# Matrix product with row normalisation: reordering VectorE's work around the start of the first two-block group

## The chip, the core and the metric

The kernel runs on one core of a Trainium2 chip. The metric is the device time of one execution in microseconds (us). A kernel's time is the median of its runs.

Engine names in the profile: PE is TensorE (matmuls), DVE is VectorE, ACT is ScalarE, POOL is GpSimd, and SPq is the queue on which SyncE issues DMAs.

## The reference

```python
def reference(a, b, gamma, eps):          # a, b: 2048 x 2048 fp32, gamma: 2048
    x = np.matmul(a, b)
    rms = np.sqrt(np.mean(x ** 2, axis=-1, keepdims=True) + eps)
    return (gamma * x / rms).astype(np.float32)
```

## The kernel before

The rows of `a` are 16 blocks of 128. A head computes blocks 0 to 3 while `b` arrives. From block 4 on the blocks go in groups of two (group 2 is blocks 4 and 5, and is called the first group, `G0`). Each half of a group's columns is computed with seven products in place of eight, in the manner of Strassen. A product is 8 matmuls of 128x512. Its left operand is either a quarter of the transposed block or a sum of two quarters (`s_1`, `s_2`, `s_5`, `s_6`, `s_7`, made on VectorE by `a_sums`). Blocks 2 and 3, called "the pair", already use the seven products for their right half. Their last additions are left over for the first group's time.

Each row block also needs a norm (`row_norm`, ScalarE), a factor from it (`row_factor`, VectorE), a scaling to fp16 (`row_apply`, ScalarE) and a transpose by DMA. Each engine works through its instructions in order. A hook is a place between two products where other work is put into the program. This is the end of the head:

```python
    p6 = new_bank()
    product(PAIR, 1, 6, p6)
    a_sums(G0, (5,))
    nc.vector.tensor_tensor(out=x22, in0=pair[1], in1=x22, op=ALU.subtract)
    for g in range(2):
        turn(HB + 1, g)                                     # TensorE transposes block 5
        take_transposed(HB + 1, g, turned[HB + 1, g], nc.vector.tensor_copy)
    square_half(0, 1)                                       # ScalarE
    square_half(1, 1)
    take_rms(0)                                             # VectorE sum (tot), ScalarE root (rms)
    a_sums(G0, (2, 1))

    def pair_sums():                                        # two additions of 128x512
        ...
    def pair_ends():                                        # two more; they empty p7 and p6
        ...
```

One half of a group, with the hooks:

```python
        product(g, j, *one)
        nc.scalar.copy(out=c, in_=one[1])                   # L591
        last_squares()
        at_hook(1)
        product(g, j, *two)
        nc.vector.tensor_tensor(out=t, in0=two[1], in1=c, op=ALU.add)      # L595
        at_hook(2)
        ...                                                 # product 1; L599
        product(g, j, 4, p2, start=False)                   # accumulates onto one/two's banks
        nc.scalar.copy(out=x21, in_=p2)                     # L602
        ...
        product(g, j, 3, p5, start=False)
        nc.scalar.copy(out=x12, in_=p5)                     # L607
        ...
```

The hooks of the first group that matter here (`nxt` is block 6). The second list belongs to its second half:

```python
            if g == G0:                                     # first half
                hook(0, finish, 0, (1,))                    # scale by gamma/rms, store
                hook(1, row_norm, nxt)
                hook(1, take_rms, 1)
                hook(2, row_factor, nxt)
                hook(2, finish, 0, (0,))
                hook(2, apply, nxt)                         # row_apply, then the transposing DMA
                hook(2, row_norm, nxt + 1)
                hook(2, a_sums, g, (7, 6))
                hook(2, finish, 1, (1, 0))
                hook(2, row_factor, nxt + 1)
                hook(2, pair_sums)
                hook(2, pair_ends)
                hook(4, apply, nxt + 1)
...
                hook(2, finish, r2, (1, 0))                 # second half: block 2's two stores
...
                hook(0, load_after, g, nxt + 2)             # load block 8, released by block 7's transpose
                if g == G0:
                    hook(2, wait_for, x_slot[HB + r2][:, 0:1])
                    hook(2, load_block, nxt + 3)            # load block 9
                    hook(5, row_norm, nxt + 2)              # norm of block 8, before the next group's L591
```

## Time and profile before

| | before |
|---|---|
| time, median of 3 runs (range) | 221.73 us (221.34 to 221.86) |
| span of the profiled run | 219.9 us |
| TensorE busy | 209.3 us (95%) |
| TensorE's one wait between 54 and 95 us | 0.5 us, for the sum `s_2` |

TensorE is the engine to watch. Once the first group runs, every product follows the last without a gap, and each takes 1.73 us (8 matmuls, 216 ns apart). A start that comes later than the previous start plus 1.73 us is therefore a wait. That is a stricter reading than the bracketed idle time, because a matmul's record lasts longer than its slot.

The prediction shows the lines around the one wait. First, ScalarE in order of time (start, length, engine, line, operation, tiles, and in brackets the idle time before it with what ended it):

```profile
91.24 1.06 ACT L219 ACTIVATE sq<-a 128x1024 bf16<-128x1024 f32 x1 [1.37 <-DMA a<-in_a_dram]
...
93.80 0.57 ACT L591 COPY x<-acc 128x512 f32<-128x512 f32 x1
```

L591 is the copy that the next group's fourth product needs. TensorE reaches that product here:

```profile
96.96 3.62 PE L285 MATMUL acc<-t_left,head_at 128*128 128x512 bf16 x16
```

### The profile page before, as it was taken

To read this page: it belongs to the slowest core of one execution; us is meant where nothing else is said; L and a number is where in the kernel's file an instruction comes from. 1 tells how busy PE (TensorE), PEld (TensorE's weight loads), DVE (VectorE), ACT (ScalarE), POOL (GpSimd) and SP (SyncE) were. 2 spreads that over 40 slices of the span, in tenths; PEclk is the share of its full clock that TensorE was granted. 3 is DMA by queue.
4 is the path that set the end of the run, shared out by engine and by line. 5 is a ranking of instruction groups with operands and counts; after the bars stand their busy time and mean duration, and the time that the engine had idled before them with its cause. 6 is when DMAs were issued, how large, how long until landed. Compare 5 with 4: busy or idle time off the path is not lost.

```text
span 219.9 us, 3044 instructions
## 1 busy us (share of the span) xinstructions
PE 209.3 (95%) x1032; PEld 97.4 (44%) x1032; DVE 165.9 (75%) x326; ACT 127.0 (58%) x263; POOL 36.3 (16%) x75
## 2 busy tenths in 40 slices
PE   7799999999999999999999999999999999999970
PEld 3344544444454444444444444444444444444440
DVE  1128799999889999979795639946695659787781
ACT  2110002920599898688745997289747996334471
POOL 7544443343020002100200002000200000000040
PEclk9999999999999999999999999999999999999996
DMA  7999999999929895948799049965699249145045
GB/s 157 164 203 206 199 206 208 212 206 228 409 76 362 291 293 118 358 176 230 213 300 405 3 93 265 351 247 95 156 294 405 42 100 364 73 174 210 1 171 212
DMA packets 36864, 46.60 MB, mean 212 GB/s; under 512 B 22256, under 2 KB 26352, under 8 KB 35568
## 3 DMA queue, kind: packets, MB, share of 16 engines
q0 software_dynamic: 10608, 23.86, 44.1%
q1 hardware_dynamic: 25824, 22.02, 33.5%
q10 hardware_dynamic: 416, 0.52, 0.7%
q8 instruction: 8, 0.13, 0.2%
q14 instruction: 8, 0.07, 0.1%
HBM read 34.60 MB, written 16.78 MB: 234 GB/s over the span
## 4 chain that ended last, share of the span: by engine, by line
PE 65%; DMA 23%; ACT 4%; POOL 2%; issue 1%; DVE 1%; ACTq 0%; POOLq 0%
PE acc L285 64%; DMA b<-in_b_dram 14%; DMA early<-in_a_dram 5%; DMA a<-in_a_dram 4%; ACT sq L219 2%; POOL b L102 1%; ACT at_even L192 1%; PE acc L790 1%; POOL early L106 1%; DVE s L260 1%; DVE at_even L192 0%; ACT x L729 0%; DVE x L551 0%; ACT norm L222 0%; ACT x L531 0%
## 5 line engine op out<-in xcount | busy, mean ns | idle before, releaser
L285 PE MATMUL acc<-b,s 128*128 128x512 bf16 x408 | 93.3, 379 | 0.5 <-DVE s L260 0.5
L285 PEld LDWEIGHTS <-s 128*128 128x128 f16 (+1 forms) x512 | 49.9, 98 | 60.4 <-DVE s L260 1.0
L388 PE MATMUL acc<-b,head_at 128*128 128x512 bf16 x176 | 43.2, 379 | 1.2 <-DMA b<-in_b_dram 1.2
L303 ACT ACTIVATE sq<-x 128x512 bf16<-128x512 f32 x53 | 33.4, 630 | 6.9 <-DVE x L722 3.0
L370 DVE SCALAR_TENSOR_TENSOR x<-x,r,gamma_sb 128x1024 f32<-128x1024 f32 x28 | 34.8, 1282 | 0.7
L219 ACT ACTIVATE sq<-a 128x1024 bf16<-128x1024 f32 x24 | 25.3, 1053 | 2.1 <-DMA a<-in_a_dram 1.5
L388 PEld LDWEIGHTS <-head_at 128*128 128x128 bf16 x176 | 16.9, 98 | 20.6 <-issue 1.6
L242 ACT ACTIVATE head_at<-a,s 128x2048 f16<-128x2048 f32 x10 | 20.0, 1998 | 3.3 <-DVE s L229 3.3
L102 POOL DMA_DIRECT2D b<-in_b_dram x32 | 17.2, 540 | 20.8 <-DMA b<-in_b_dram 15.0
L430 ACT COPY x<-acc 128x512 f32<-128x512 f32 x5 | 2.9, 582 | 24.7 <-PE acc L388 24.7
L285 PEld LDWEIGHTS <-head_at 128*128 128x128 f16 (+1 forms) x112 | 10.9, 98 | 13.2
L285 PE MATMUL acc<-early,head_at 128*128 128x512 bf16 x64 | 14.5, 379 | 0.0
L285 PEld LDWEIGHTS <-at_even 128*128 128x128 f16 x96 | 9.4, 98 | 11.3
L285 PE MATMUL acc<-early,s 128*128 128x512 bf16 x56 | 14.2, 379 | 0.0
L260 DVE TENSOR_TENSOR s<-head_at 128x1024 f16<-128x1024 f16 (+5 forms) x22 | 13.4, 635 | 0.1
L609 DVE TENSOR_TENSOR x<-x,x 128x512 f32<-128x512 f32 x9 | 6.2, 692 | 8.8 <-ACT x L607 8.3
L127 POOL COPY pace<-x 128x1 f32<-128x1 f32 x4 | 1.7, 413 | 66.7 <-DVE x L618 65.6
L591 ACT COPY x<-acc 128x512 f32<-128x512 f32 x9 | 5.2, 573 | 11.5 <-PE acc L285 11.5
L173 DVE COPY head_at<-tbank 128x1024 bf16<-128x1024 bf16 x7 | 4.8, 692 | 8.7 <-PE tbank L168 8.5
L285 PE MATMUL acc<-t_left,s 128*128 128x512 bf16 x48 | 11.3, 379 | 0.0
L774 POOL TENSOR_SCALAR x<-x,r 128x512 f32<-128x512 f32 x1 | 2.7, 2652 | 51.2 <-DVE r L346 51.2
L276 DVE TENSOR_TENSOR b<-b 128x1024 bf16<-128x1024 bf16 x16 | 10.8, 684 | 0.2
(113 smaller groups left out, 237.5 us busy)
## 6 DMA issues: line engine op xcount, KB each, us to landing
out_dram<-x SPq DMA_DIRECT2D x29, 512.0 KB, 3.8
a<-in_a_dram POOLq DMA_DIRECT2D x10, 1024.0 KB, 8.7
b<-in_b_dram POOLq DMA_DIRECT2D x32, 256.0 KB, 10.0
a<-in_a_dram POOLq DMA_DIRECT2D x4, 512.0 KB, 9.8
early<-in_a_dram POOLq DMA_DIRECT2D x7, 256.0 KB, 10.2
gamma_sb<-in_gamma_dram POOLq DMA_DIRECT2D x2, 512.0 KB, 8.3
out_dram<-x SPq DMA_DIRECT2D x3, 256.0 KB, 2.6
out_dram<-a SPq DMA_DIRECT2D x1, 512.0 KB, 3.3
```

Of the source, the lines that this page charges most:

```text
L102: nc.gpsimd.dma_start(out=raw[j][kp][:, t, :], in_=b[lo:lo + P, j * HALF:(j + 1) * HALF])
L173: nc.vector.tensor_copy(out=head_at[:, 2 * kp:2 * kp + 2, :, :], in_=view)
L219: nc.scalar.activation(out=junk, in_=a32[mb][:, h * HALF:(h + 1) * HALF], func=ACTF.Square, scale=2.0 ** -8, accum_out=n2[:, h:h + 1])
L242: nc.scalar.activation(out=a16[mb], in_=a32.pop(mb), func=ACTF.Copy, scale=factor.pop(mb))
L260: nc.vector.tensor_tensor(out=sum_of(g, s)[:, lo:hi, :], in0=x[:, lo:hi, :], in1=y[:, lo:hi, :], op=op)
L276: nc.vector.tensor_tensor(out=flat[:, 1:3, :], in0=flat[:, 1:3, :], in1=flat[:, 0::3, :], op=ALU.add)
L285: nc.tensor.matmul(bank, lhsT[:, kp, :], rhs, start=(start and kp == 0), stop=(kp == KP - 1), skip_group_check=not start)
L303: nc.scalar.activation(out=sq[:, 0:CH], in_=src, func=ACTF.Square, scale=inv_sqrt_n, accum_out=msq[mb][:, c:c + 1])
L370: nc.vector.scalar_tensor_tensor(out=x, in0=x, scalar=inverse_of[mb], in1=gamma_sb[:, h * HALF:(h + 1) * HALF], op0=ALU.mult, op1=ALU.mult)
L388: nc.tensor.matmul(bank, head_at[:, kt, r, :], head_rhs(c, kt), start=(kt == 0), stop=(kt == KT - 1))
L591: nc.scalar.copy(out=c, in_=one[1])
L609: nc.vector.tensor_tensor(out=t, in0=t, in1=x12, op=ALU.add)
```

## The change

The intent: let VectorE do the two sums that TensorE waits for before a subtraction that nobody waits for; use VectorE's wait for the next norm for the pair's sums; empty the pair's two banks sooner.

```diff
     a_sums(G0, (5,))
-    nc.vector.tensor_tensor(out=x22, in0=pair[1], in1=x22, op=ALU.subtract)
     for g in range(2):
         turn(HB + 1, g)
         take_transposed(HB + 1, g, turned[HB + 1, g], nc.vector.tensor_copy)
     square_half(0, 1)
     square_half(1, 1)
+    a_sums(G0, (2, 1))
+    nc.vector.tensor_tensor(out=x22, in0=pair[1], in1=x22, op=ALU.subtract)
     take_rms(0)
-    a_sums(G0, (2, 1))
...
                 hook(1, take_rms, 1)
+                hook(2, pair_sums)
                 hook(2, row_factor, nxt)
-                hook(2, finish, 0, (0,))
                 hook(2, apply, nxt)
                 hook(2, row_norm, nxt + 1)
                 hook(2, a_sums, g, (7, 6))
-                hook(2, finish, 1, (1, 0))
+                hook(2, pair_ends)
+                hook(2, finish, 0, (0,))
+                hook(2, finish, 1, (1,))
                 hook(2, row_factor, nxt + 1)
-                hook(2, pair_sums)
-                hook(2, pair_ends)
+                hook(2, finish, 1, (0,))
```

## The prediction

> **What bounds the kernel now.** I read the busy times first, then the chain that ended last, then TensorE's waits, and then the order of time around the one place where TensorE waits. The page's first part:
>
> ```profile
> PE 209.3 (95%) x1032; PEld 97.4 (44%) x1032; DVE 165.9 (75%) x326; ACT 127.0 (58%) x263; POOL 36.3 (16%) x75
> ```
>
> The last pieces of the chain before its long end (start, length, what; us):
>
> ```profile
> 68.54 0.06 DVE tot L335
> 68.60 0.67 DVE s L260
> 69.27 0.05 issue
> 69.32 141.76 PE acc L285 x656
> ```
>
> From 69.32 on, the chain is TensorE alone: 656 matmuls without one step to another engine. 141.76/656 is 216.1 ns each. The pace without waits can be read at the two products that start at 84.87 and end where the next starts at 88.32: 3.45 us for 16, or 215.6 ns. At that pace 656 would take 141.4 us, so at most 0.3 us of stall lies in all of that stretch. Whatever happens to VectorE and ScalarE after 69.32 is hidden as long as no matmul waits for it. TensorE's waits from 54 to 95 us have a single entry:
>
> ```profile
> PE acc L285 <- DVE s L260: 0.5, 1, 0.5
> ```
>
> In TensorE's order of time it is this (s_5's product of the first group, then s_2's, then s_1's, then two on the transposed block):
>
> ```profile
> 66.97 1.89 PE L285 MATMUL acc<-b,s 128*128 128x512 bf16 x8
> 69.32 1.90 PE L285 MATMUL acc<-b,s 128*128 128x512 bf16 x8 [0.46 <-DVE s L260]
> 71.06 1.89 PE L285 MATMUL acc<-t_left,s 128*128 128x512 bf16 x8
> 72.78 0.59 PE L285 MATMUL acc<-t_left,at_even 128*128 128x512 bf16 x2
> ```
>
> Eight matmuls from 66.97 at 0.2157 end their issue at 68.70; the next begins at 69.32. So the true loss is 0.62 us (the record shows 0.46 because a matmul's record outlasts its slot). That is the prize. VectorE there:
>
> ```profile
> 66.05 0.69 DVE L260 TENSOR_TENSOR s<-at_even 128x1024 f16<-128x1024 f16 x1 [0.21 <-ACT at_even L192]
> 66.66 0.68 DVE L551 TENSOR_TENSOR x<-acc,x 128x512 f32<-128x512 f32 x1
> 67.26 0.68 DVE L192 COPY at_even<-tbank 128x1024 f16<-128x1024 f16 x1
> 67.86 0.68 DVE L192 COPY at_even<-acc 128x1024 f16<-128x1024 f16 x1
> 68.46 0.14 DVE L335 TENSOR_REDUCE tot<-msq 128x1 f32<-128x5 f32 x1
> 68.57 1.29 DVE L260 TENSOR_TENSOR s<-at_even 128x1024 f16<-128x1024 f16 x2
> 69.78 0.16 DVE L346 RECIPROCAL r<-rms 128x1 f32<-128x1 f32 x1
> 69.97 1.28 DVE L370 SCALAR_TENSOR_TENSOR x<-x,r,gamma_sb 128x1024 f32<-128x1024 f32 x1
> 71.18 0.15 DVE L335 TENSOR_REDUCE tot<-msq 128x1 f32<-128x5 f32 x1
> 71.33 0.69 DVE L595 TENSOR_TENSOR t_first<-acc,head_at 128x512 f32<-128x512 f32 x1
> ```
>
> VectorE is never idle here, so anything put ahead of something else delays the latter by its step. Steps: 0.60 from one of these sums or copies to the next, 0.71 where it reads what its predecessor wrote (the two pair sums start at 78.46 and 79.17), 1.21 after a scaling of 128x1024.
>
> **What the Trainium skill says.** "TensorE: Matmul & The Clock Gate", section "Wait — 56ns, not 53.3ns?": 512-column matmuls start 215.7 ns apart when warm; the trace's 215.6 agrees, so TensorE has no slower pace to mend. "VectorE: DVE Perf Modes", section "The DRAIN you can't avoid": a semaphore between two instructions costs nothing extra. Here it differs: 0.71 against 0.60, and I use the trace. "Perfetto Trace Analysis", section "Matmuls": rotate groups through banks so that emptying one overlaps the next. The trace agrees that this works already: the pair's seventh product sits in its bank from 64 us until 79.78 (the first of the sums that end the pair) and TensorE never waits for it. Same page, section on DMA instructions of the Sync queue: the record covers the issue, not the data. Here the store issued at 71.29 has a record of 0.35 us and lands after 4.1.
>
> **The change, part by part.** No instruction is added or removed; 286 VectorE rows stand in both builds. TensorE's own order is the same. Three moves:
>
> (1) Head's end: s_2 and s_1 go ahead of the subtraction (L551) and of the row-0 sum of squares (tot).
> (2) Inside the group: the two pair sums go ahead of the next row factor, and the two pair ends ahead of three scalings.
> (3) On the Sync queue the transposing DMA of block 6 now comes before the store of row 0's left half, which came before it.
>
> (1) worked out. s_5 stays at 66.05. The first copy now waits for the transposes, whose records end at 66.68: 66.72. Second copy 67.32. s_2 reads it: +0.71, 68.03, done 68.71. The second product starts at about 68.78 instead of 69.32: gain 0.54, remaining wait 0.08. Then s_1 68.64, subtraction 69.25, tot 69.85 (before: 68.46). ScalarE takes row 0's root only after tot: 70.03 to 70.23 (before 68.64). So the reciprocal is at 70.27, the scaling 70.46, the second tot 71.67, and L595 runs 71.82 to 72.51 (before 71.33 to 72.02). L595 empties the bank onto which the fourth product accumulates. TensorE would be ready for that product at 68.78 + 2 x 1.73 = 72.24, but gets the bank at 72.57: a new wait of 0.33. Before it started at 72.78. The gain is now 0.21.
>
> (2) and ScalarE. ScalarE also loses 1.39 at that root, because its copy (L591), two squares and norm stand behind it in order. These are the lines that it then works through without a break:
>
> ```profile
> 72.64 2.00 ACT L242 ACTIVATE head_at<-a,s 128x2048 f16<-128x2048 f32 x1 [0.52 <-DVE s L229]
> 78.33 2.00 ACT L242 ACTIVATE head_at<-a,s 128x2048 f16<-128x2048 f32 x1
> 82.64 0.57 ACT L591 COPY x<-acc 128x512 f32<-128x512 f32 x1
> ```
>
> The pair sums (72.42, 73.13) fill VectorE until the norm, now at about 73.4; the factor's third step ends at 74.26, where it ended at 72.60. ScalarE's first L242 starts at 74.30 instead of 72.64, and all behind it shifts by 1.66. On VectorE s_7 and s_6 come at 74.43 and 75.03 (product 7 wants them at 76.03: fine), the pair ends at 75.64 and 76.24, scalings at 76.85 and 78.24, the second factor done 79.98: second L242 at 80.02 (+1.69). So L591, which copies the second half's first product, runs 84.33 to 84.90. That bank is wanted by the fourth product of the second half; before, TensorE started it at 84.87 with ScalarE done at 83.21. After, TensorE would be ready at 72.57 + 7 x 1.726 = 84.65 and starts at 84.95. So the 0.21 is gone again, and 0.08 more.
>
> (3) The store of row 0's left half is scaled at 76.85 to 78.13 and its SBUF half is written next by ScalarE's L607, which would come at 81.92. The Sync queue issues in order. Before, the block-6 transpose held it for 3.18 us (74.67 to 77.85, with a store in flight), elsewhere 1.9. It now starts at 76.33, so the store goes out between 78.3 and 79.6 and lands 2.9 to 3.5 us later, between 81.2 and 83. L607 is late by 0 to 1.1; I take 0.1 to 0.2, as fewer transfers are in flight at 76. That adds to the wait of L591.
>
> Sum: 0.62 removed; 0.08 + 0.33 + 0.30 + 0.15 = 0.86 new. Net +0.2 us: 221.73 + 0.2 = 221.9. After that the lag of 1.7 us drains where ScalarE waits anyway (the before trace shows it waiting 1.37 at 91.24, 2.10 at 110.97, 3.84 at 117.88), and TensorE's fourth product at 96.96 has its copy done at 94.37, 2.6 us ahead. The 7 us after the last matmul are untouched.
>
> **Rivals.** First, the intended one: the wait goes and nothing replaces it. Then 221.73 - 0.54 = 221.2. For it: the only recorded wait of TensorE vanishes. Against it: L595 had only 72.78 - 72.02 = 0.76 of slack, and loses 0.49 while TensorE comes 0.54 earlier. Second, the store is blocked by the transpose as long as before (3.18): L607 at 82.5, L591 at 84.9, TensorE at 85.55, 0.7 later than before: 222.4. If the block-7 transpose, now right behind the store of row 1, also lands late, the load behind it and row 8's norm delay the copy for the product at 96.96 by up to the 2.6 us slack: up to 0.5 more, 222.9. Third, earlier freed banks matter: speaks against it that no product waited for one of them; worth 0.
>
> **Range and chances.** The floor is 221.2 less a little run-to-run scatter (221.34 to 221.86 before); the blocked store gives the ceiling. Range 221.2 to 222.7. Two per cent is 4.4 us, seven times the whole wait at stake, so within 2% is nearly certain: 0.98, 0.01 on each side.
>
> **What would show it.** Right: no wait, or under 0.15, before s_2's product; a wait of about 0.3 before the fourth product with L595 as releaser; ScalarE's first L242 near 74.3; a wait for ScalarE's L591 near 84.9. Wrong: TensorE with no wait after 68.8 (then my VectorE steps are too long and the time is 221.2), or the root of row 0 not moved by 1.4 us, or L607 waiting for the store well past 82.5 (then 222.4 or more).

## The result and the profile after

The changed kernel takes 224.44 us (median of 6 runs, 224.08 to 225.27), against 221.73 us for the kernel before (6 runs, 221.34 to 223.81). The ratio is 1.0116, with a 95% interval of 1.0074 to 1.0157. The prediction was 221.9 us, with a range of 221.2 to 222.7. It was wrong: the time lies 1.7 us above the range. That the change would stay within 2% held (1.2%), but not for the reason given, the size of the wait at stake: a loss is not bounded by the wait that was to be removed, and 2.7 us are four times the 0.62. The profiled spans, 222.6 and 219.9 us, show the same difference of 2.7 us.

The page's first part shows almost no difference in work:

```profile
PE 209.8 (94%) x1032; PEld 97.5 (44%) x1032; DVE 166.0 (75%) x326; ACT 126.7 (57%) x263; POOL 36.2 (16%) x75
```

So the 2.7 us are waiting. TensorE's waits from 66 to 120 us (who waited for whom: total, times, longest):

```profile
PE acc L285 <- ACT x L591: 2.0, 2, 1.7
PE acc L285 <- DVE s L227: 0.3, 1, 0.3
```

The wait for `s_2` is gone from the list (about 0.1 us of it is left: the two products from 66.91 take 3.57 us, where 3.45 would do), and two new releasers have taken its place. TensorE in order of time:

```profile
70.48 1.89 PE L285 MATMUL acc<-t_left,s 128*128 128x512 bf16 x8
72.42 3.61 PE L285 MATMUL acc<-t_left,at_even 128*128 128x512 bf16 x16
...
84.90 3.61 PE L285 MATMUL acc<-early,at_even 128*128 128x512 bf16 x16 [0.22 <-ACT x L591]
...
98.89 1.89 PE L285 MATMUL acc<-t_left,head_at 128*128 128x512 bf16 x8 [1.74 <-ACT x L591]
101.07 1.89 PE L285 MATMUL acc<-t_left,head_at 128*128 128x512 bf16 x8 [0.30 <-DVE s L227]
```

Compare starts with the kernel before. At the fourth product of the second half TensorE is at 84.90, where it was at 84.87: nothing lost and nothing gained so far. At the next group's fourth product it is at 98.89 instead of 96.96, 1.93 us late. The next product begins 2.18 us after that instead of 1.73, so 0.45 more. (The releaser named there, L227, is the instruction behind L595, which empties this product's bank from 100.32 to 101.01 and was itself late.) A last 0.3 us is lost in that group's second half: its fourth product starts 2.02 us after the third (109.70 and 111.72) instead of 1.72. The sum is 0.03 + 1.90 + 0.45 + 0.30 = 2.68 us, which is the whole difference of the spans.

The chain that ended last says where the 1.9 us come from (start, length, what):

```profile
87.31 0.51 POOL pace L127
87.82 7.80 DMA a<-in_a_dram
95.66 0.04 issue
95.71 1.16 ACT sq L219 x2
...
98.27 0.56 ACT x L591
```

The chain runs from the load of block 8 (released on GpSimd) through the norm of that block into the copy L591, and then into TensorE. ScalarE's own order of time shows how it got there:

```profile
69.98 0.20 ACT L337 ACTIVATE rms<-tot 128x1 f32<-128x1 f32 x1 [1.56 <-DVE tot L335]
...
74.18 2.00 ACT L242 ACTIVATE head_at<-a,s 128x2048 f16<-128x2048 f32 x1 [0.87 <-DVE s L229]
...
84.28 0.56 ACT L591 COPY x<-acc 128x512 f32<-128x512 f32 x1
...
95.71 1.06 ACT L219 ACTIVATE sq<-a 128x1024 bf16<-128x1024 f32 x1 [5.82 <-DMA a<-in_a_dram]
...
98.27 0.56 ACT L591 COPY x<-acc 128x512 f32<-128x512 f32 x1
```

ScalarE is 1.3 to 1.6 us late up to 84.28, as predicted. Then it waits 5.82 us for a load that before cost it 1.37, and is 4.5 us late. The copy at 84.28 costs TensorE what it had gained; the last line costs it 1.9 us more.

Why did the load come so late? In the kernel before, GpSimd issues it alone, and block 2's first store follows on the Sync queue 1.5 us later:

```profile
85.53 0.53 POOL L121 DMA_DIRECT2D a<-in_a_dram  x1 [0.32 <-ACT rms L337]
```

```profile
87.05 1.53 SPq L376 DMA_DIRECT2D out_dram<-x  x2
```

In the changed kernel both are issued in the same 0.04 us:

```profile
87.82 0.53 POOL L121 DMA_DIRECT2D a<-in_a_dram  x1
```

```profile
87.86 1.53 SPq L376 DMA_DIRECT2D out_dram<-x  x2
```

The DMA view of a stretch says what moved in it (queue, kind: packets, MB, share of 16 engines). Before, from 87 to 90 us, only the software queue, which carries the loads, moved data:

```profile
q0 software_dynamic: 110, 0.90, 82.2%
```

After, from 88 to 90 us, only the hardware queue, which carries the stores, moved data:

```profile
q1 hardware_dynamic: 112, 0.46, 71.9%
```

The store overtook the load. Issued with 1.5 us of lead, the load moved its first packet 1.24 us after its issue and landed after 5.6 us; it was the store that then moved nothing for 3.04 us. Issued side by side with the store, the load moved its first packet only after 2.71 us, the store's coming after 0.83, and it landed after 7.8. So 1.5 of the 2.2 us are a later first packet. With the 2.29 us of later issue (85.53 to 87.82) that makes 4.5 us, and TensorE's slack at that point was 2.6.

### The profile page after: what moved, and what is told of

The parts are those of the page before. It is cut to its first block, busy times and chain, and to the rows that moved or that the text cites. A ratio compares the mean times of both kernels' runs of the same rounds, so it can differ in the third digit from the quotient of the medians. Undisturbed runs are those within 1.5% of the kernel's fastest.

```text
span 222.6 us, 3042 instructions
## 1 busy us (share of the span) xinstructions
PE 209.8 (94%) x1032; PEld 97.5 (44%) x1032; DVE 166.0 (75%) x326; ACT 126.7 (57%) x263; POOL 36.2 (16%) x75
## 4 chain that ended last, share of the span: by engine, by line
PE 51%; DMA 26%; issue 12%; ACT 4%; POOL 3%; DVE 2%; POOLq 0%; ACTq 0%
PE acc L285 50%; DMA b<-in_b_dram 13%; DMA a<-in_a_dram 8%; DMA early<-in_a_dram 5%; ACT sq L219 2%; POOL b L102 1%; PE acc L791 1%; ACT sq L303 1%; POOL early L106 1%; DVE gamma_sb L240 1%; ACT x L591 0%; POOL a L121 0%; ACT x L730 0%; DVE x L595 0%; DVE b L276 0%
## 5 line engine op out<-in xcount | busy, mean ns | idle before, releaser
L285 PE MATMUL acc<-b,s 128*128 128x512 bf16 x408 | 93.2, 379 | 0.0
L285 PEld LDWEIGHTS <-s 128*128 128x128 f16 (+1 forms) x512 | 49.9, 98 | 59.9 <-DVE s L260 0.4
L242 ACT ACTIVATE head_at<-a,s 128x2048 f16<-128x2048 f32 x10 | 20.0, 1998 | 3.7 <-DVE s L229 3.7
L285 PEld LDWEIGHTS <-head_at 128*128 128x128 f16 (+1 forms) x112 | 10.9, 98 | 15.9 <-issue 3.0
L285 PEld LDWEIGHTS <-at_even 128*128 128x128 f16 x96 | 9.4, 98 | 11.9 <-issue 0.8
L285 PE MATMUL acc<-early,head_at 128*128 128x512 bf16 x64 | 14.5, 379 | 0.1
L285 PE MATMUL acc<-early,s 128*128 128x512 bf16 x56 | 14.2, 379 | 0.0
L285 PE MATMUL acc<-t_left,head_at 128*128 128x512 bf16 x48 | 11.0, 379 | 2.0 <-ACT x L591 1.7
L591 ACT COPY x<-acc 128x512 f32<-128x512 f32 x9 | 5.1, 572 | 11.5 <-PE acc L285 7.6
L285 PE MATMUL acc<-t_left,s 128*128 128x512 bf16 x48 | 11.3, 379 | 0.0
L285 PE MATMUL acc<-early,at_even 128*128 128x512 bf16 x48 | 10.8, 379 | 0.2 <-ACT x L591 0.2
```

What stands on the lines that cost most here:

```text
L242: nc.scalar.activation(out=a16[mb], in_=a32.pop(mb), func=ACTF.Copy, scale=factor.pop(mb))
L285: nc.tensor.matmul(bank, lhsT[:, kp, :], rhs, start=(start and kp == 0), stop=(kp == KP - 1), skip_group_check=not start)
```

## The experiments

The theory: the loss of 2.7 us is ScalarE's lag of some 1.6 us, turned into a load that is late and loses its lead over a store, and carried back to TensorE because the norm of block 8 stands ahead of the copy L591. The rivals: the late root of row 0 at the head's end is to blame by itself; the other banks that the products got are to blame; the stores behind the transpose on the Sync queue are to blame. Every kernel gave correct results, and each experiment was timed in 5 rounds. "Stretch" below is the time from the start of the first group's first product (66.97 in the kernel before) to the start of the next group's fourth (96.96), read from the traces. It leaves out how fast the head was in a given run. The lead is that over block 2's first store.

| kernel | time, median | before, same rounds | ratio (95% interval) | stretch | load issued ahead of store | load lands after |
|---|---|---|---|---|---|---|
| before | 221.73 | | | 29.99 | 1.52 | 5.6 |
| after | 224.44 | 221.73 | 1.0116 (1.0074 to 1.0157) | 31.98 | 0.04 | 7.8 |
| x1_head | 222.18 | 221.55 | 1.0032 (1.0013 to 1.0051) | 30.33 | 1.47 | 6.3 |
| x2_hooks | 223.88 | 221.55 | 1.0115 (1.0088 to 1.0141) | 31.47 | 0.04 | 8.0 |
| x3_norm_late | 222.08 | 221.55 | 1.0028 (1.0010 to 1.0046) | 30.05 | 0.03 | 7.8 |
| x4_load_early | 221.86 | 221.55 | 1.0014 (0.9996 to 1.0031) | 30.07 | 6.98 | 7.1 |
| x6_second_load_late | 231.54 | 221.66 | 1.0442 (1.0396 to 1.0487) | 33.17 | 0.03 | 8.5 |
| x7_root_early | 221.19 | 221.66 | 0.9970 (0.9925 to 1.0014) | 29.46 | 1.74 | 6.0 |
| x8_root_and_load_early | 221.22 | 221.66 | 0.9987 (0.9934 to 1.0040) | 29.46 | 5.92 | 8.4 |
| x9_load_lead | 222.25 | 221.98 | 1.0013 (0.9992 to 1.0034) | 30.06 | 2.71 | 6.1 |
| x7_again | 221.11 | 221.98 | 0.9973 (0.9953 to 0.9994) | 29.46 | 1.73 | 5.2 |

### One part at a time: x1_head and x2_hooks

x1_head is the kernel before with the first hunk of the change alone, x2_hooks the one with the second hunk alone.

```diff
 x1_head:
-    nc.vector.tensor_tensor(out=x22, in0=pair[1], in1=x22, op=ALU.subtract)
...
+    a_sums(G0, (2, 1))
+    nc.vector.tensor_tensor(out=x22, in0=pair[1], in1=x22, op=ALU.subtract)
     take_rms(0)
-    a_sums(G0, (2, 1))
 x2_hooks:
+                hook(2, pair_sums)
                 hook(2, row_factor, nxt)
-                hook(2, finish, 0, (0,))
...                 (and the rest of the second hunk)
```

> The head's move alone (sums of rows 2 and 3's products ahead of the subtraction and of row 0's sum of squares), the group's order as before. Theory (the loss is ScalarE's lag, carried by the load of row block 8 to the copy L591 of the next group; it takes both moves to make the lag long enough): ScalarE's first L242 comes near 73.8 instead of 74.2, the load is issued near 86.7 and still lands ahead of need, no wait near 97; TensorE keeps part of the gain: 221.3 to 221.6. Rival A (the late root of row 0 alone is the cause): 223.5 or more. Rival B (changed banks are the cause): banks of the group are as before here, so 221.2.

> The group's reorder alone, the head as before. Theory: ScalarE's first L242 near 73.8 (pair sums put 1.3 us ahead of the factor), the second one near 79.5, the load of block 8 issued near 87.1 with the two stores at the same time, landing 7 to 8 us later; the copy L591 of the next group comes late and TensorE waits 0.4 to 1.5 us near 97; 222.2 to 223.6. Rival A (the head's late root is the cause): 221.7. Rival B (banks): 224.4, as the banks are those of the changed kernel.

x1_head took 222.18 us. That is far from the 224.4 of the whole change, so the late root of row 0 (70.00 here, 68.64 before) is not the cause by itself. The load kept its lead, and there was no wait near 97. But the expected gain did not come either: it is 0.6 us slower than before. The stretch is 0.34 us longer. Its largest wait, which I had not foreseen, is new:

```profile
PE acc L285 <- DVE x L565: 0.5, 1, 0.5
```

L565 is the first of the pair's ends. It empties the bank of the pair's seventh product, which the second half's second product takes. L565 comes 1.21 us later than before (80.99 instead of 79.78), and TensorE is ready for the bank about 0.3 us earlier (near 81.09 instead of 81.42), so that bank comes too late. So the second hunk's early emptying has a purpose once the first hunk is in. My prediction had called it worth nothing.

x2_hooks took 223.88 us, 0.3 above the expected range: the load was issued at 87.20, the store at 87.24, the load landed after 8.0 us, and TensorE waited 1.64 us for L591 near 98. The second hunk alone makes most of the loss. Its mechanism is the pair sums put ahead of the row factor: ScalarE's first L242 starts at 73.57 instead of 72.64, after a wait of 1.38 us for the factor.

The two runs together correct the theory: the length of ScalarE's lag is not what decides. At the first L242 x1_head lags by 1.20 us and loses nothing near 97, while x2_hooks lags by 0.93 and loses most of it. What differs is the lead. In x1_head VectorE is late too, so the load and block 2's store, whose scaling VectorE makes, both come 1.2 to 1.3 us later than before. In x2_hooks the load comes 1.67 us later and the store only 0.19. Of the 1.67, 0.93 are ScalarE's lag and 0.7 the slower landing of block 7's transpose. That transpose landed after 5.3 to 5.4 us in the changed kernel, x2_hooks and x3_norm_late, where row 1's last store is issued 0.6 us before it, and after 4.6 to 4.7 in the kernel before and x1_head, where that distance is 1.8.

### The load's place on ScalarE: x3_norm_late

The changed kernel, with the norm of block 8 behind the copy.

```diff
                 if g == G0 + 1:
                     done.insert(0, r3)
-                else:
-                    hook(1, row_norm, nxt)
+                hook(1, row_norm, nxt)
...
-                    hook(5, row_norm, nxt + 2)
```

> The changed kernel, but the norm of row block 8 stands on ScalarE behind the copy L591 of the next group instead of ahead of it. The load still lands near 95.7. Theory: L591 comes near 93.6, the waits of 1.74 and 0.30 us near 97 and 101 vanish, 222.0 to 222.5 (if the norm's lateness turns up nowhere else). Rivals (banks, stores behind the transpose on the Sync queue): no change, 224.4.

It took 222.08 us. The load was as late as in the changed kernel (issued 87.92, landing after 7.8), and the copy L591 waited for TensorE alone:

```profile
93.83 0.58 ACT L591 COPY x<-acc 128x512 f32<-128x512 f32 x1 [3.84 <-PE acc L285]
```

TensorE's fourth product started at 97.08, and the waits of 1.74 and 0.30 us were gone. Banks, stores and the order on the Sync queue were those of the changed kernel. So the late load costs TensorE nearly all of its time through the order on ScalarE, and the two rivals fall. The time stays 0.5 us above the kernel before of the same rounds, and the interval holds that apart from zero. The trace shows 0.2 us of it: 0.06 in the stretch and 0.14 before the fourth product of the next group's second half (107.44 to 109.31).

### The load's time: x4_load_early and x9_load_lead

The changed kernel, with the load of block 8 released by block 6's transpose (x4_load_early), or by the second half's first copy (x9_load_lead).

```diff
 x4_load_early, in load_after:
-        wait_for(at(2 * g + 3)[:, KT - 1, 0:1] if g == G0 else ...)
+        wait_for(at(2 * g + 2)[:, KT - 1, 0:1] if g == G0 else ...)
 x9_load_lead, in load_after and in the hooks:
-        wait_for(at(2 * g + 3)[:, KT - 1, 0:1] if g == G0 else ...)
+        wait_for(x_chunk(2 * g + 1, 3)[:, 0:1] if g == G0 else ...)
-                hook(0, load_after, g, nxt + 2)
+                hook(1 if g == G0 else 0, load_after, g, nxt + 2)
```

> The changed kernel, but the load of row block 8 waits for block 6's transpose instead of block 7's, so it is issued near 81 instead of 87.8. Theory: it lands before 89, the norm is done before the copy L591 is wanted, no wait near 97: 221.8 to 222.3. Rival (the wait comes from ScalarE's own lag, not from the load): L591 at most 1.7 us earlier, TensorE still waits, 223.5 or more. Rival banks: 224.4.

> The changed kernel, with one wait exchanged: the load of row block 8 is released by the second half's first copy (L591, done near 84.9) instead of by block 7's transpose, so it is issued near 85.5, some 2 us ahead of the store near 87.9, where the changed kernel has 0.04 us. ScalarE, VectorE and the Sync queue keep their late order. Theory (the lost lead over the store is what costs the load its time): it lands 5.5 to 7 us later, by 92.5, and TensorE has no wait near 97: 221.7 to 222.3. If the load is slow for another reason (the second load, the transposes): it lands after 94 and a wait of 0.5 to 1.5 stays, 223 or more.

x4_load_early took 221.86 us. The load was issued at 81.55 and landed after 7.1 us, long before it was needed. (Here too a store, one of row 1, was issued 0.04 us behind the load, and the load's first packet came only after 3.5 us.) The wait near 97 was gone, with ScalarE's lag still in place: its first L242 started at 74.47, its second-half copy at 84.56, and TensorE still waited 0.23 us for that copy.

x9_load_lead moves the release only as far as the kernel before had it: the load was issued at 85.60, 2.71 us ahead of the store at 88.31. It landed after 6.1 us instead of 7.8, and ScalarE's wait for it was nearly that of the kernel before (1.37):

```profile
91.75 1.06 ACT L219 ACTIVATE sq<-a 128x1024 bf16<-128x1024 f32 x1 [1.41 <-DMA a<-in_a_dram]
```

The same two stores and the same second load follow in this kernel. So the lost lead over the store is what lengthened the load. (A lead is not enough where other transfers are in flight: the load of x8_root_and_load_early, below, took 8.4 us with block 7's transpose issued 0.6 us ahead of it and a store 1.25 us behind it.) Its time of 222.25 us lies 0.3 above the kernel before, which its interval does not tell from zero.

### The second load: x6_second_load_late

The changed kernel, with the load of block 9 held back to the end of the second half.

```diff
-                    hook(2, wait_for, x_slot[HB + r2][:, 0:1])
-                    hook(2, load_block, nxt + 3)
+                    hook(7, wait_for, x_chunk(2 * g + 1, 3)[:, 0:1])
+                    hook(7, load_block, nxt + 3)
```

> The changed kernel, with the load of row block 9 held back to near 95, so that block 8's load (issued near 87.8) shares the DMA engines with the two stores only. If the second load is what slows the first: it lands after 5.6 to 6.5 us instead of 7.8, TensorE's wait near 97 shrinks from 1.74 to 0 to 0.7, 222.6 to 223.4. If the two stores alone slow it: landing still 7.5 to 8, no change, 224.4 less at most 0.2. If the late block 9 hurts in its turn, waits appear after 105.

The load of block 8 landed after 8.5 us although nothing but the two stores ran beside it until 96. The second load is thus not what slows the first. Nor is it other work on GpSimd, which does nothing from 89.64 to 96.07: the load, issued at 89.11, again moved nothing at first. From 89.7 to 91.7 us this is all that moved:

```profile
q1 hardware_dynamic: 129, 0.50, 81.5%
```

The time, 231.54 us, was a miss: I had not expected a new loss of 7 us. Holding back block 9 puts the later groups behind. The largest of the new waits on ScalarE is one of 9.3 us, for a store into whose buffer it copies:

```profile
ACT x L591 <- DMA out_dram<-x: 9.3, 1, 9.3
```

I did not take that loss apart further. It belongs to the experiment, not to the change.

### A version meant to beat both: x7_root_early, x8_root_and_load_early, x7_again

If the head's gain is real, it can be had without ScalarE's lag. x7_root_early makes `s_2` first and row 0's sum of squares right behind it, then `s_1`. The subtraction goes behind L595, and the pair's ends go ahead of one scaling only. The store of that scaling is issued behind block 7's transpose, so that it does not hold up the transpose on the Sync queue.

```diff
     square_half(1, 1)
+    a_sums(G0, (2,))
     take_rms(0)
-    a_sums(G0, (2, 1))
+    a_sums(G0, (1,))
...
+                hook(2, pair_difference)              # the subtraction
                 hook(2, row_factor, nxt)
                 hook(2, finish, 0, (0,))
...
-                hook(2, finish, 1, (1, 0))
+                hook(2, finish, 1, (1,))
+                hook(2, pair_sums)
                 hook(2, row_factor, nxt + 1)
-                hook(2, pair_sums)
                 hook(2, pair_ends)
+                hook(2, scale, 1, (0,))
                 hook(4, apply, nxt + 1)
+                hook(4, store, 1, (0,))
```

> A version that should beat both: s_2's sum first, row 0's sum of squares right behind it (so ScalarE's root stays near 68.8), then s_1; the subtraction behind the first emptying L595; the pair's ends ahead of the last scaling only; the last store of row 1 behind block 7's transpose. Theory: no wait before s_2's product beyond 0.1, none before the fourth product, ScalarE's first L242 near 72.8, the load issued near 85.8, no wait near 97: 0.4 to 0.6 us under the kernel before of the same rounds. If instead the lost 0.6 us always returns as another wait: equal to the kernel before.

> x7 with the load of row block 8 waiting for block 6's transpose, as in the early-load run. If x7 leaves any wait near 97, this removes it; if not, it equals x7 (0.4 to 0.6 us under the kernel before), as TensorE has no wait left there.

> The same kernel as x7_root_early once more, for the interval: 0.3 to 0.6 us under the kernel before of the same rounds (ratio 0.997 to 0.9985).

The diff above is against the kernel before. x7_again is the same kernel once more, run at another time. x8_root_and_load_early adds the release of x4_load_early to it:

```diff
-        wait_for(at(2 * g + 3)[:, KT - 1, 0:1] if g == G0 else ...)
+        wait_for(at(2 * g + 2)[:, KT - 1, 0:1] if g == G0 else ...)
```

x7_root_early took 221.19 us against 221.66, and the repeat 221.11 against 221.98. The first interval (0.9925 to 1.0014) holds 1; the second (0.9953 to 0.9994) does not. The repeat's 0.87 us between the medians is more than the 0.3 to 0.6 expected; its ratio of 0.9973, 0.6 us, is inside. In both traces the stretch is 29.46 us against 29.99: 0.53 of the 0.62 us that were at stake, and the gain lasts to the end: from the first group's first product to the start of the last L285 matmul they take 143.2 us, the kernel before 143.7. TensorE from the first group's first product on, in x7_root_early:

```profile
66.99 3.73 PE L285 MATMUL acc<-b,s 128*128 128x512 bf16 x15
70.55 1.89 PE L285 MATMUL acc<-t_left,s 128*128 128x512 bf16 x8
72.28 3.62 PE L285 MATMUL acc<-t_left,at_even 128*128 128x512 bf16 x16
```

Two products from 66.99 would take 3.45 us and take 3.56; the next takes 1.73. ScalarE's root was at 68.86, its first L242 at 72.70, the load had its lead and landed after 6.0 us. x8_root_and_load_early has the same stretch, as expected, and 221.22 us. With the load early it lost 0.27 us elsewhere, before the next group's second half's fourth product (106.97 to 108.96), so in the traces x7 is the better of the two; the times do not tell them apart.

## Why the prediction was wrong

**The bound and the prize.** Right. TensorE bounds the stretch, and 0.62 us was at stake. x7_root_early takes 0.53 of it.

**(1), the head.** Right to within 0.15 us. Predicted and measured: the root of row 0 at 70.03 and 69.98, L595 from 71.82 and 71.69, the fourth product at 72.57 and 72.42. The new wait there was 0.2 us instead of 0.33.

**(2), ScalarE's lag.** Right. First L242 at 74.30 and 74.18, second at 80.02 and 79.87, L591 at 84.33 and 84.28, the second half's fourth product at 84.95 and 84.90. The statement "the 0.21 is gone again, and 0.08 more" came out as 0.03, or 0.09 counted from the first group's first product.

**Small slips in the reading.** The steps of 0.71 and 0.60 held, but the second pair sum does not read the first one's result: it overwrites one of its inputs. "Elsewhere 1.9" for a transpose's hold of the queue leaves out block 7's, 2.48. And the profiles have 326 VectorE instructions in both builds; I found no view that gives 286. None of these moved the sum.

**(3), the blocked store.** Right in direction, and harmless. The transpose held the queue for 2.04 us, the store went out at 78.31 and landed after 3.5 us, and L607 started at 81.85 without a wait. The 0.15 us that I added for it were not there.

**The step that failed** is the one after the sum: "After that the lag of 1.7 us drains where ScalarE waits anyway (the before trace shows it waiting 1.37 at 91.24 ...), and TensorE's fourth product at 96.96 has its copy done at 94.37, 2.6 us ahead." The wait of 1.37 us is a wait for the load of block 8. That load is released by block 7's transpose, which is released by the second L242, which is itself part of the lagging chain. A wait for something that the lag itself delays does not drain the lag. The terms that I set to zero there measured: the transpose issued 1.55 us later (80.35 and 81.90), landing 0.7 us slower, and the load 2.2 us slower because the store overtook it. Together 4.5 us, against a slack of 2.6. What followed was 1.9 us at the fourth product, 0.45 at the one after, and 0.3 in that group's second half. The table shows it by taking single links out: x4_load_early and x9_load_lead remove the lateness of the load, x3_norm_late its way to TensorE, and in all three the stretch falls back to 30.05 to 30.07 us, within 0.1 of the kernel before.

The prediction's four signs of being right came (the second as 0.2 us, too short for the list of waits to name L595), and none of its signs of being wrong: it watched for nothing after 85 us, where the loss was.

**The rivals.** The second one named this very path: block 7's transpose lands late behind a store (it did, by 0.7 us), and "the load behind it and row 8's norm delay the copy". But it bounded the path by "up to 0.5 more", and it added it only to a blocked store that was not blocked. Here the mechanism was right and the size wrong: ScalarE's own lag in front of the transpose was left out, and the load's duration was taken from the before trace as if nothing would share its start. The third rival, that earlier freed banks are worth 0, holds for the kernel before, where no product waited for one. It is refuted with the first hunk in: x1_head waits 0.46 us for such a bank.

What stays open: why a load with a store beside it moves nothing at first. Where the store was issued within 0.04 us behind the load, its first packet came 2.7 to 3.5 us after its issue (after, x2_hooks, x3_norm_late, x4_load_early, x6_second_load_late); with 1.5 us of lead or more it came after 1.2 to 1.6 (before, x1_head, x9_load_lead, both runs of x7_root_early). The idle GpSimd of x6_second_load_late rules out its other instructions as the reason. Also open is the rest of x1_head's loss: its stretch accounts for 0.34 of 0.6 us, and no run here tells the remainder from scatter.

## What to carry to other kernels

A lag on an engine off the critical path is drained only by waits on things that the lag does not delay. For each wait counted as slack, follow the releaser back to see whether it hangs on the lagging engine itself. Where the chain passes through a DMA, look at what else is issued in the same microsecond: a transfer's duration in the old trace holds only for the old order of issue. That order can hang on two engines, here the load on ScalarE and the store on VectorE: a lag of both kept it, a lag of one lost it. And when an instruction is moved ahead to help one engine, check which result it now delays for a third; here a reduction of 0.14 us behind three others kept ScalarE waiting for 1.6.

## What the Trainium skill lacked or had wrong

- "VectorE: DVE Perf Modes", section "The DRAIN you can't avoid", has a semaphore between two VectorE instructions cost nothing extra. In these traces independent instructions of 128x512 and 128x1024 start 0.60 us apart. One that reads its predecessor's result starts 0.71 us after it (changed kernel: the second copy at 67.28 and `s_2` at 67.99) or 0.77 (before: L599 at 80.98 and L604 at 81.75), and one that overwrites its predecessor's input 0.71 (before: the pair sums at 78.46 and 79.17). No run here tells whether a semaphore takes the difference.
- "DMA: Bandwidth & Descriptors", section "Queues, rings and completion order", says that each engine goes round-robin between its queues at packet granularity, which reads as if two transfers issued close together shared the time. Here the one that came first kept the other out for 2 to 3 us: the store from 88 to 90 us in the changed kernel (0.46 MB against none), the load from 87 to 90 in the kernel before (0.90 MB against none, with the store issued at 87.05). The traces do not show when each queue's descriptors were ready, so this need not contradict the page.
- "Advanced Engine Details and Errata", section "DGE: Hardware vs Software", gives about 1 us to the first byte for GpSimd's descriptors and about 600 ns for the Sync queue's. The order agrees: 1.24 us for the load in the kernel before and 0.83 for the store in the changed kernel, each with no other transfer in flight that had begun to move. What the table lacks is a neighbour: beside that store the load took 2.71 us, and behind the load the store of the kernel before took 3.04.
- No page that I used says how long a transposing DMA holds its issuing queue when other transfers run. Transposes of one block held the Sync queue 2.04 us in the changed kernel with few transfers in flight (block 6), 3.63 us with stores just issued (block 7), and 6.25 us in x4_load_early with a load issued beside it (block 7).
